# A chunked recurrence whose heads move from chunk-dependent to parity-dependent partitions, with the output normalization queued one chunk later

## The chip, the cores and the metric

The kernel runs on one core of one Trainium2 chip. The metric is the device time of one execution in microseconds (us), the lower the better. All work is in fp32, with bulk matmuls split into a rounded high part and a rest (three matmuls for one product).

## The reference, cut to what matters

Two transformer-like blocks run one after the other on 512 positions of width 1024. The first has an RWKV-7 branch with 8 heads of 64; this recurrence is what the change touches:

```python
def step(state, inp):                     # per head, state S is 64 x 64
    r_t, w_t, k_t, v_t, a_t, b_t = inp
    sa = einsum("bhvk,bhk->bhv", state, a_t)
    state = state * w_t[:, :, None, :] + sa[..., None] * b_t[:, :, None, :] + v_t[..., None] * k_t[:, :, None, :]
    return state, einsum("bhvk,bhk->bhv", state, r_t)
...
y = (y - mu) * rsqrt(var + LN_X_EPS)      # normalized over the 64 of each head
y = y.reshape(bsz, s, D_RWKV) * ln_x_w + ln_x_b
y = y + bonus                             # sum(r * k * r_k) * v per head
return y * g
```

After it come a convolution branch, gates, cross attention to 256 memory rows, an MLP, and the second block (windowed attention, a gated unit, projections).

## The kernel before, in words

The framework orders the instructions of each engine from a plan with estimated durations; each engine then runs its own queue in that order. TensorE's queue therefore mixes the scan's small matmuls with the bulk matmuls (lines 193 to 195) of projections that do not need the scan. Bulk weights are loaded by SyncE's queue (L185), cast on ScalarE (L167) and their rest is formed on VectorE (L168).

The recurrence is computed in 8 chunks of 64 positions, two to a block `tb` of 128. For each chunk `gram` (L441) forms the products within the chunk for all 8 heads; `inverse` (L453) solves the small triangular systems for both chunks of a block on VectorE, 31 steps, with transposes through DRAM (`md`, `M`, `zd`, `ZT`, 16 transfers on SyncE's queue). `chunk` (L490) then goes through these steps, each for 8 heads or 4 head pairs: right-hand sides (L502, and L506 from the carried state), a first solve with 32x32 blocks (L517), the coupling (L521), a second solve (L526), the state update (L533) and the output (L547 from the state, L550 from within the chunk). Between them ScalarE copies right-hand sides out of PSUM (`gsb`), VectorE copies solutions into `VU` and updates the state. `VU` holds values and solutions: for even chunks the values lie on partitions 0 to 63 and the solutions on 64 to 127, for odd chunks the other way round:

```python
kb, ub = 64 * c, 64 * (1 - c)             # c = n % 2
...
PE.matmul(pg[ub:ub + 64, hd * 64:(hd + 1) * 64], lhsT=gr[:, hd, 0:64], rhs=VU[:, tb, c, hd, :], ...)
```

So within a chunk all heads write the same 64 output partitions. An fp32 matmul appears in the trace as two records. `post(tb)` normalizes the output of a block; it follows the block's second chunk. `gt` (gates) takes the result, is transposed at L666 and feeds `ya`. The pool `t` (function `tt`) has ten slots and serves most temporaries.

Of the kernel before, what the change touches and what calls it, by code (L numbers as in the profile page):

```python
# [22 lines left out]
TB = 4  # L23
# [23 lines left out]
def fused_kernel(ctx, tc, a, out):  # L47
# [274 lines left out]
    PC = tp.tile([128, 8, 8], F32, tag="PC", name="PC")  # L322
    G.memset(VU[64:128, :, 0], 0.0)
    G.memset(VU[0:64, :, 1], 0.0)
    bon = tp.tile([128, TB, 8], F32, tag="bon", name="bon")
# [11 lines left out]

    def halves(ap):
        return ap.rearrange("p (m x) -> p m x", x=128)

    def prep(j, tail):
# [7 lines left out]
        for tb in range(TB):  # L349
# [16 lines left out]
        G.tensor_tensor(PC[:, :, 2 * j:2 * j + 2], pp[:, :, 64:65].to_broadcast([128, 8, 2]),  # L366
                        hsel.unsqueeze(1).to_broadcast([128, 8, 2]), op=ALU.mult)
# [13 lines left out]
        kb = KB[:, j].rearrange("p (m x) -> p m x", x=256)  # L381
# [13 lines left out]
    def prep_tail(j, rkk, vs):  # L395
        pb = scbank()
        for tb in range(TB):
            PE.matmul(pb[:, 2 * tb:2 * tb + 2], lhsT=rkk[:, tb * 128:(tb + 1) * 128], rhs=hsel, start=True, stop=True)
        V.tensor_copy(bon[:, :, 2 * j:2 * j + 2], pb[:, 0:8].rearrange("p (t q) -> p t q", q=2))
        pv = scbank()  # L400
        for tb in range(TB):
            PE.transpose(pv[:, tb * 128:(tb + 1) * 128], vs[:, tb * 128:(tb + 1) * 128], ident)
        for c in range(2):
            S.copy(VU[64 * c:64 * c + 64, :, c, 2 * j:2 * j + 2, :],
                   pv[64 * c:64 * c + 64].rearrange("p (t h n) -> p t h n", t=TB, h=2))
# [31 lines left out]
    nc.sync.dma_start(lnx[:, 0], a["ln_x_w"][0:1, :].partition_broadcast(128))  # L437
    nc.sync.dma_start(lnx[:, 1], a["ln_x_b"][0:1, :].partition_broadcast(128))
    lnw, lnb = lnx[:, 0], lnx[:, 1]
    def gram(n):  # L440
        t = reg.tile([128, 8, 128], F32, tag="G4", bufs=4, name=nm("gram"))  # L441
        pq = [scbank(), scbank()]
        for hd in range(8):
            j, p0 = hd // 2, 64 * (hd % 2)
            PE.matmul(pq[hd % 2][:, j * 128:(j + 1) * 128], lhsT=KB[p0:p0 + 64, j, n * 128:(n + 1) * 128],  # L445
                      rhs=AR[p0:p0 + 64, j, n].rearrange("p q c -> p (q c)"), start=True, stop=True)
        tv = t.rearrange("p (j q) c -> p q j c", q=2)
# [5 lines left out]
    def inverse(grams):  # L453
        md = dr.tile([32, 32, 32], F32, tag="md", bufs=2, name=nm("md"))
        for i in range(2):
            ub = 64 * (1 - i)
            for d in range(2):
                q0 = (i * 2 + d) * 8
                nc.sync.dma_start(md[q0:q0 + 8].rearrange("h j i -> j h i"),
                                  grams[i][ub + 32 * d:ub + 32 * d + 32, :, 32 * d:32 * d + 32])  # L460
# [18 lines left out]
        ZT = tt("ZT", (128, 2, 8, 32))  # L479
        for i in range(2):  # L480
            ub = 64 * (1 - i)
            for d in range(2):
                q0 = (i * 2 + d) * 8
                nc.sync.dma_start(ZT[ub + 32 * d:ub + 32 * d + 32, i], zd[q0:q0 + 8].rearrange("h c i -> c h i"))
        return ZT

    state = [None]
    ybank = [None]

    def chunk(n, gr, ZT):  # L490
        tb, c = n // 2, n % 2
        kb, ub = 64 * c, 64 * (1 - c)
        sp = state[0]
# [7 lines left out]
        for hd in range(8):  # L501
            PE.matmul(pg[ub:ub + 64, hd * 64:(hd + 1) * 64], lhsT=gr[:, hd, 0:64],  # L502
                      rhs=VU[:, tb, c, hd, :], start=hd == 0, stop=n == 0 and hd == 7)
        if n > 0:
            for j in range(4):
                PE.matmul(pg[ub:ub + 64, j * 128:(j + 1) * 128], lhsT=AR[:, j, n, 0, :],  # L506
                          rhs=sp[:, j, :], start=False, stop=j == 3)
        if 0 < n < 7:
            spc = tt("spc", (128, 4, 128))
            G.tensor_tensor(spc.rearrange("p j (q v) -> p (j q) v", q=2), sp.rearrange("p j (q v) -> p (j q) v", q=2),  # L510
                            PC[:, n, :].unsqueeze(2).to_broadcast([128, 8, 64]), op=ALU.mult)
        gsb = tt("gsb")
        pu = chbank()
        S.copy(gsb[ub:ub + 32], pg[ub:ub + 32])
        for hd in range(8):
            hs = slice(hd * 64, (hd + 1) * 64)
            PE.matmul(pu[ub:ub + 32, hs], lhsT=ZT[ub:ub + 32, c, hd, :], rhs=gsb[ub:ub + 32, hs],  # L517
                      start=True, stop=True)
        V.tensor_copy(VU[ub:ub + 32, tb, c], pu[ub:ub + 32].rearrange("p (h v) -> p h v", v=64))
        for hd in range(8):  # L520
            PE.matmul(pg[ub + 32:ub + 64, hd * 64:(hd + 1) * 64], lhsT=gr[ub:ub + 32, hd, 32:64],  # L521
                      rhs=VU[ub:ub + 32, tb, c, hd, :], start=False, stop=hd == 7, skip_group_check=True)
        S.copy(gsb[ub + 32:ub + 64], pg[ub + 32:ub + 64])
        for hd in range(8):
            hs = slice(hd * 64, (hd + 1) * 64)
            PE.matmul(pu[ub + 32:ub + 64, hs], lhsT=ZT[ub + 32:ub + 64, c, hd, :], rhs=gsb[ub + 32:ub + 64, hs],  # L526
                      start=True, stop=True)
        V.tensor_copy(VU[ub + 32:ub + 64, tb, c], pu[ub + 32:ub + 64].rearrange("p (h v) -> p h v", v=64))

        if n < 7:  # L530
            pst = chbank()
            for j in range(4):
                PE.matmul(pst[:, j * 128:(j + 1) * 128], lhsT=KBt[:, 2 * j:2 * j + 2, :].rearrange("p h f -> p (h f)"),  # L533
                          rhs=VU[:, tb, c, 2 * j:2 * j + 2, :].rearrange("p h v -> p (h v)"),
                          start=j == 0, stop=j == 3)
            sn = tmp("state", (128, 4, 128), bufs=2)
            V.tensor_tensor(sn.rearrange("p j (q v) -> p (j q) v", q=2), pst.rearrange("p (jq v) -> p jq v", v=64),
                            PC[:, n, :].unsqueeze(2).to_broadcast([128, 8, 64]), op=ALU.mult)
            if n > 0:
                V.tensor_tensor(sn, sn, spc, op=ALU.add)  # L540
            state[0] = sn
        if c == 0:
            ybank[0] = chbank()
        py = ybank[0]
        if n > 0:
            for j in range(4):
                PE.matmul(py[kb:kb + 64, j * 128:(j + 1) * 128], lhsT=AR[:, j, n, 1, :],  # L547
                          rhs=sp[:, j, :], start=j == 0, stop=False)
        for hd in range(8):
            PE.matmul(py[kb:kb + 64, hd * 64:(hd + 1) * 64], lhsT=gr[:, hd, 64:128], rhs=VU[:, tb, c, hd, :],  # L550
                      start=n == 0 and hd == 0, stop=hd == 7)
# [4 lines left out]
    def post(tb):  # L556
        y = tt("y")
        S.copy(y, ybank[0])
        bv = tt("bv")
        for c in range(2):  # L560
            rows = slice(64 * c, 64 * c + 64)
            G.tensor_tensor(heads(bv[rows]), VU[rows, tb, c], bon[rows, tb, :].unsqueeze(2).to_broadcast([64, 8, 64]),
                            op=ALU.mult)
# [38 lines left out]
    scan_front(0)  # L602
    for tb in range(TB):
        if tb < TB - 1:
            scan_front(tb + 1)
        for c in range(2):
# [51 lines left out]
    for j in range(DB):  # L658
# [3 lines left out]
        if j % 2 == 0:  # L662
# [5 lines left out]
            split(p.rearrange("p (j t) -> p j t", t=128), ya[:, :, 0, ts_], ya[:, :, 1, ts_])  # L668
# [511 lines left out]
for _name, _n in VSIZE:  # L1180
# [4 lines left out]
    "mem", "w_lora_w", "w_lora_a", "w_lora_g", "ln_x_w", "ln_x_b", "norm_mem", "norm_final",  # L1185
# [15 lines left out]
def _layout(inputs):  # L1201
# [26 lines left out]
    r["w_v"] = _half_tiles(g["w_kv"][0][:, D:])  # L1228
    w2 = g["w_in_2"][0]
# [27 lines left out]
```

## Time and profile before

| | us |
|---|---|
| median of 3 runs | 1328.11 |
| lowest and highest run | 1325.77, 1330.02 |
| the profiled execution | 1321.5 |
| its span | 1319.5 |
| TensorE busy in it | 1290.2 (98%) |
| VectorE, ScalarE, GpSimd busy | 829.1, 530.4, 166.3 |

A profile shows one execution. Busy time is by engine (PE is TensorE's matmuls, PEld its weight loads, DVE VectorE, ACT ScalarE, POOL GpSimd, SP SyncE); idle time of an engine that is not the bottleneck costs nothing. Matmuls are pipelined: a record's length holds its passage through the array, and the distance from start to start tells what it occupies.

### The profile page before, as it was taken

The page shows a single profiled execution, that of the slowest core. Times are in us where ns is not written, and L with a number is a line of the kernel's source. Part 1 is how long each engine was busy: PE and PEld are TensorE (multiplying, and loading weights), DVE is VectorE, ACT ScalarE, POOL GpSimd, SP SyncE. Part 2 cuts the span into 40 slices and gives each one's busy share as a digit, 9 for nine tenths or more (in the row PEclk, how much of TensorE's full clock was granted, in tenths as well). Part 3 has the DMA queues.
Part 4 walks back from the last instruction along what each step waited for, and adds up shares of the span by engine and source line. Part 5 has one row for each costly group of instructions (what it writes and reads, how often), then busy time and mean ns, then how long its engine had stood idle before and what let it go on. Part 6 is the DMA issues. An engine that isn't in the chain of part 4 may idle for free.

```text
span 1319.5 us, 18273 instructions
## 1 busy us (share of the span) xinstructions
PE 1290.2 (98%) x6594; PEld 1061.5 (80%) x6594; DVE 829.1 (63%) x1657; ACT 530.4 (40%) x956; POOL 166.3 (13%) x178
## 2 busy tenths in 40 slices
PE   8989999999999999999999999999999999999997
PEld 6778888878889888888888888888878777788886
DVE  6867585857477665656845636544677666663356
ACT  6534332322344443544523323324345465333342
POOL 1222101020110020002021020120232000100003
PEclk9989999999999999999999999999999999999999
DMA  6111432323324522143544535323334223233331
GB/s 233 56 56 59 115 102 67 98 59 115 95 66 137 195 98 83 56 161 122 190 128 129 191 97 165 110 92 96 96 120 143 74 70 130 88 96 97 97 118 64
DMA packets 85498, 143.95 MB, mean 109 GB/s; under 512 B 21504, under 2 KB 21632, under 8 KB 85408
## 3 DMA queue, kind: packets, MB, share of 16 engines
q1 hardware_dynamic: 85408, 142.78, 34.7%
q8 instruction: 52, 0.85, 0.3%
q14 instruction: 38, 0.31, 0.1%
HBM read 136.19 MB, written 5.24 MB: 107 GB/s over the span
## 4 chain that ended last, share of the span: by engine, by line
PE 93%; DVE 5%; issue 1%; POOL 0%; DMA 0%; ACT 0%; SPq 0%; DVEq 0%; ACTq 0%; POOLq 0%
PE mm L193 25%; PE mm L194 25%; PE mm L195 25%; PE mm L686 1%; PE mm L687 1%; PE mm L685 1%; PE sc L445 1%; DVE wlo L168 1%; PE ch L1046 1%; PE ch L517 1%; PE ch L1011 1%; PE ch L550 1%; PE ch L521 1%; PE ch L526 1%; PE ch L502 1%
## 5 line engine op out<-in xcount | busy, mean ns | idle before, releaser
L167 ACT CAST whi<-wraw 128x512 fp32r<-128x512 f32 x398 | 246.5, 622 | 518.7 <-PE mm L194 452.8
L168 DVE TENSOR_TENSOR wlo<-wraw,whi 128x512 fp32r<-128x512 f32 x398 | 291.4, 734 | 206.7 <-PE mm L195 105.4
L193 PE MATMUL mm<-h,whi 128*128 128x512 f32 x296 | 118.3, 400 | 0.0
L194 PE MATMUL mm<-h,whi 128*128 128x512 f32 x296 | 117.1, 396 | 0.0
L195 PE MATMUL mm<-h,wlo 128*128 128x512 f32 x296 | 116.6, 394 | 0.0
L193 PE MATMUL mm<-x2g,whi 128*128 128x512 f32 x256 | 100.2, 391 | 0.0
L195 PE MATMUL mm<-x2g,wlo 128*128 128x512 f32 x256 | 99.7, 390 | 0.0
L194 PE MATMUL mm<-x2g,whi 128*128 128x512 f32 x256 | 99.6, 389 | 0.0
L193 PE MATMUL mm<-ff,whi 128*128 128x512 f32 x256 | 99.6, 389 | 0.0
L194 PE MATMUL mm<-ff,whi 128*128 128x512 f32 x256 | 99.6, 389 | 0.0
L195 PE MATMUL mm<-ff,wlo 128*128 128x512 f32 x256 | 99.6, 389 | 0.0
L910 POOL TENSOR_TENSOR X<-X,d 128x512 f32<-128x512 f32 x24 | 39.3, 1636 | 220.9 <-DVE d L908 220.9
L193 PEld LDWEIGHTS mm<-h,whi 128*128 128x128 f32 x296 | 55.9, 189 | 13.6 <-DVE k L287 1.1
L195 PEld LDWEIGHTS mm<-h,wlo 128*128 128x128 f32 x296 | 55.9, 189 | 11.8 <-issue 0.2
L194 PEld LDWEIGHTS mm<-h,whi 128*128 128x128 f32 x296 | 55.9, 189 | 11.2 <-issue 0.2
L716 POOL TENSOR_TENSOR gt<-gt,nsq 128x512 f32<-128x512 f32 x21 | 27.7, 1321 | 274.9 <-ACT nsq L715 267.4
L194 PE MATMUL mm<-h2a,whi 128*128 128x512 f32 x152 | 59.8, 393 | 0.5 <-DVE h2a L933 0.5
L193 PE MATMUL mm<-h2a,whi 128*128 128x512 f32 x152 | 59.4, 393 | 0.3 <-ACT h2a L932 0.3
L195 PE MATMUL mm<-h2a,wlo 128*128 128x512 f32 x152 | 59.7, 393 | 0.0
L193 PE MATMUL mm<-h2b,whi 128*128 128x512 f32 x152 | 59.6, 392 | 0.0
L195 PE MATMUL mm<-h2b,wlo 128*128 128x512 f32 x152 | 59.5, 392 | 0.0
L194 PE MATMUL mm<-h2b,whi 128*128 128x512 f32 x152 | 59.3, 391 | 0.0
(488 smaller groups left out, 2777.7 us busy)
## 6 DMA issues: line engine op xcount, KB each, us to landing
wraw<-in_w_in SPq DMA_DIRECT2D x162, 256.0 KB, 2.7
wraw<-in_w_up SPq DMA_DIRECT2D x64, 256.0 KB, 2.6
wraw<-in_w_down SPq DMA_DIRECT2D x64, 256.0 KB, 2.7
adaraw<-in_w_ada SPq DMA_DIRECT2D x24, 512.0 KB, 3.6
wraw<-in_w_proj_b SPq DMA_DIRECT2D x16, 256.0 KB, 2.6
wraw<-in_w_k SPq DMA_DIRECT2D x16, 256.0 KB, 2.7
wraw<-in_w_proj_a SPq DMA_DIRECT2D x16, 256.0 KB, 2.8
wraw<-in_w_v SPq DMA_DIRECT2D x16, 256.0 KB, 2.7
```

The costliest lines, as they stand in the source:

```text
L167: S.copy(hi, src)
L168: eng.tensor_tensor(lo, src, hi.bitcast(F32), op=ALU.subtract)
L193: PE.matmul(acc, lhsT=wh, rhs=xh, start=start and k == 0, stop=False)
L194: PE.matmul(acc, lhsT=wh, rhs=xl, start=False, stop=False)
L195: PE.matmul(acc, lhsT=wl, rhs=xh, start=False, stop=stop and k == n - 1)
L445: PE.matmul(pq[hd % 2][:, j * 128:(j + 1) * 128], lhsT=KB[p0:p0 + 64, j, n * 128:(n + 1) * 128], rhs=AR[p0:p0 + 64, j, n].rearrange("p q c ...
L502: PE.matmul(pg[ub:ub + 64, hd * 64:(hd + 1) * 64], lhsT=gr[:, hd, 0:64], rhs=VU[:, tb, c, hd, :], start=hd == 0, stop=n == 0 and hd == 7)
L517: PE.matmul(pu[ub:ub + 32, hs], lhsT=ZT[ub:ub + 32, c, hd, :], rhs=gsb[ub:ub + 32, hs], start=True, stop=True)
L521: PE.matmul(pg[ub + 32:ub + 64, hd * 64:(hd + 1) * 64], lhsT=gr[ub:ub + 32, hd, 32:64], rhs=VU[ub:ub + 32, tb, c, hd, :], start=False, sto ...
L526: PE.matmul(pu[ub + 32:ub + 64, hs], lhsT=ZT[ub + 32:ub + 64, c, hd, :], rhs=gsb[ub + 32:ub + 64, hs], start=True, stop=True)
L716: G.tensor_tensor(self.acc, self.acc, sq, op=ALU.add)
L910: G.tensor_tensor(X[:, j], X[:, j], d, op=ALU.add)
```

## The change

Heads are placed by the parity of their pair `j` (pairs 0 and 2 against 1 and 3), for all chunks alike: values of even pairs on partitions 0 to 63 and their solutions on 64 to 127, odd pairs the other way round. Each step's 8 matmuls are issued in `order8`, in which the parity changes from one to the next, so that the output half does too; the free axis of each PSUM tile is 256 columns in place of 512. The first half solution is copied by VectorE and the other by ScalarE. The state is kept in two fixed tiles whose unused blocks are zeroed once; the next chunk's decayed state is formed on GpSimd from the new sum (`cn`). `y` is copied out of PSUM per chunk. The inverse's transfers are split by parity (8 + 4 + 4 + 8 in place of 4 + 4 + 4 + 4). Gate columns and the normalization's weights are laid out by parity on the host, gates are written in four quarter copies, and `post(tb)` is queued after the first chunk of the next block; for the last block it stays behind its second chunk.

```diff
-    VU = reg.tile([128, TB, 2, 8, 64], F32, tag="R", bufs=7, name="VU")
+    VU = reg.tile([128, 8, 8, 64], F32, tag="R", bufs=7, name="VU")
...
-        V.scalar_tensor_tensor(kb[:, :, 64:192], halves(ta), 1.0, halves(m1), op0=ALU.add, op1=ALU.mult)
-        V.tensor_tensor(kb[:, :, 0:64], halves(f)[:, :, 0:64], halves(ip)[:, :, 0:64], op=ALU.mult)
-        V.tensor_tensor(kb[:, :, 192:256], halves(f)[:, :, 64:128], halves(ip)[:, :, 64:128], op=ALU.mult)
+        kb = KB[:, j].rearrange("p (n x) -> p n x", x=128)
+        ub, vb = 64 * (1 - j % 2), 64 * (j % 2)
+        V.scalar_tensor_tensor(kb[:, :, ub:ub + 64], chunks(ta), 1.0, chunks(m1), op0=ALU.add, op1=ALU.mult)
+        V.tensor_tensor(kb[:, :, vb:vb + 64], chunks(f), chunks(ip), op=ALU.mult)
...
-        S.activation(g, p, AF.Copy, scale=0.5)
+        for c in range(2):
+            for jp in range(2):
+                S.activation(g[64 * jp:64 * jp + 64, 256 * c:256 * c + 256],
+                             p[64 * c:64 * c + 64, 256 * jp:256 * jp + 256], AF.Copy, scale=0.5)
...
+    order8 = [(hp, jh, jp) for hp in range(2) for jh in range(2) for jp in range(2)]
...
+        blocks = [(i, d, jp, ((i * 2 + d) * 2 + jp) * 4, 64 * (1 - jp) + 32 * d)
+                  for i in range(2) for d in range(2) for jp in range(2)]
+        for i, d, jp, q0, r0 in blocks:
+            nc.sync.dma_start(md[q0:q0 + 4].rearrange("h j i -> j h i"),
+                              grams[i][r0:r0 + 32, 4 * jp:4 * jp + 4, 32 * d:32 * d + 32])
...
-        for hd in range(8):
-            PE.matmul(pg[ub:ub + 64, hd * 64:(hd + 1) * 64], lhsT=gr[:, hd, 0:64],
-                      rhs=VU[:, tb, c, hd, :], start=hd == 0, stop=n == 0 and hd == 7)
+        for hp, jh, jp in order8:
+            ub, b = 64 * (1 - jp), 2 * jh + hp
+            PE.matmul(pg[ub:ub + 64, b * 64:(b + 1) * 64], lhsT=gr[:, 4 * jp + b, 0:64],
+                      rhs=VU[:, n, 4 * jp + b, :], start=b == 0, stop=n == 0 and b == 3)
...
+        for d in range(2):
+            S.copy(gh[:, d], pg[:, 0:256])
+            for hp, jh, jp in order8:
+                r0, b = 64 * (1 - jp) + 32 * d, 2 * jh + hp
+                hs = slice(b * 64, (b + 1) * 64)
+                PE.matmul(pu[r0:r0 + 32, hs], lhsT=ZT[r0:r0 + 32, c, b, :], rhs=gh[r0:r0 + 32, d, hs],
+                          start=True, stop=True)
+            for jp in range(2):
+                r0 = 64 * (1 - jp) + 32 * d
+                (V.tensor_copy, S.copy)[jp](VU[r0:r0 + 32, n, 4 * jp:4 * jp + 4, :],
+                                            pu[r0:r0 + 32, 0:256].rearrange("p (h v) -> p h v", v=64))
...
+                for hp in range(2):
+                    PE.matmul(pst[64 * hp:64 * hp + 64, j * 64:(j + 1) * 64], lhsT=KBt[:, 2 * j + hp, :],
+                              rhs=VU[:, n, g0 + hp, :], start=j == 0, stop=j == 3)
...
             if n > 0:
-                V.tensor_tensor(sn, sn, spc, op=ALU.add)
-            state[0] = sn
...
+                V.tensor_tensor(s1, ps_, comp[0], op=ALU.add)
+            else:
+                V.tensor_copy(s1, ps_)
+            for hp in range(2):
+                rows = slice(64 * hp, 64 * hp + 64)
+                V.tensor_tensor(sn[rows, :, 64 * hp:64 * hp + 64], s1[rows], pc[rows], op=ALU.mult)
+            if n < 6:
+                cn = tt("cn", (128, 4, 64))
+                G.tensor_tensor(cn, s1, pc, op=ALU.mult)
+                comp[0] = cn
...
+        S.copy(y[:, 256 * c:256 * c + 256], py[:, 0:256])
...
         for c in range(2):
-            chunk(2 * tb + c, grams[tb][c], zts[tb])
-        if tb == TB - 1:
-            mem_norm()
-        post(tb)
+            chunk(2 * tb + c, grams[tb][c], zts[tb], ys[tb])
+            if tb and c == 0:
+                post(tb - 1, ys[tb - 1])
+    mem_norm()
+    post(TB - 1, ys[TB - 1])
```

## Rows read from the trace of the kernel before

**Rows 1.** The page: busy time, share of the span; the chain that ended last.
```profile
PE 1290.2 (98%) x6594; PEld 1061.5 (80%) x6594; DVE 829.1 (63%) x1657; ACT 530.4 (40%) x956; POOL 166.3 (13%) x178
...
PE 93%; DVE 5%; issue 1%; POOL 0%; DMA 0%; ACT 0%; SPq 0%; DVEq 0%; ACTq 0%; POOLq 0%
```

**Rows 2.** Windows: length, busy us of PE, PEld, DVE, ACT, POOL; granted clock, DMA.
```profile
142.00:420.00 278.00, 274.72 (x1925) 230.98 (x1925) 188.76 (x505) 91.00 (x158) 33.08 (x41) 1.00 0.33 95
208.00:232.00 24.00, 23.88 (x252) 20.15 (x253) 11.18 (x19) 5.19 (x9) 6.44 (x10) 1.00 0.17 47
```

**Rows 3.** TensorE groups by shape, 142 to 392 us: tile, shape, records, busy, mean.
```profile
L502 PE MATMUL ch<-VU,gram 128*64 128x64 f32 x128 | 8.8, 222 | 0.0
...
L517 PE MATMUL ch<-gsb,ZT 32*32 32x64 f32 x128 | 8.6, 216 | 0.0
L547 PE MATMUL ch<-state,AR 128*64 128x128 f32 x56 | 7.6, 279 | 0.0
...
L533 PE MATMUL ch<-VU,KBt 128*128 128x128 f32 x56 | 7.4, 274 | 0.0
```

**Rows 4.** TensorE's timeline, 142 to 367 us: start, length, array tile, shape, records.
```profile
142.82 1.16 PE L445 MATMUL sc<-AR,KB 64*128 64x128 f32 x16
...
208.57 1.07 PE L517 MATMUL ch<-gsb,ZT 32*32 32x64 f32 x16
215.03 1.05 PE L533 MATMUL ch<-VU,KBt 128*128 128x128 f32 x8
...
217.93 0.71 PE L506 MATMUL ch<-state,AR 128*64 128x128 f32 x5
218.37 0.32 PE L547 MATMUL ch<-state,AR 128*64 128x128 f32 x1
218.48 0.27 PE L506 MATMUL ch<-state,AR 128*64 128x128 f32 x1
...
218.75 0.71 PE L547 MATMUL ch<-state,AR 128*64 128x128 f32 x5
...
291.00 0.71 PE L445 MATMUL sc<-AR,KB 64*128 64x128 f32 x8
...
298.85 1.10 PE L502 MATMUL ch<-VU,gram 128*64 128x64 f32 x16
301.88 1.09 PE L506 MATMUL ch<-state,AR 128*64 128x128 f32 x8
...
366.42 1.07 PE L517 MATMUL ch<-gsb,ZT 32*32 32x64 f32 x16
```

**Rows 5.** Timeline of weight loads at 218.4 and 1048.3 us.
```profile
218.37 0.14 PEld L506 LDWEIGHTS ch<-state,AR 128*64 128x64 f32 x1
218.37 0.13 PEld L547 LDWEIGHTS ch<-state,AR 128*64 128x64 f32 x1
...
1048.30 0.14 PEld L1046 LDWEIGHTS ch<-apT,vtok 128*64 128x64 f32 x2 [0.36 <-ACT apT L1043]
```

**Rows 6.** VectorE's and ScalarE's groups by shape, 142 to 480 us.
```profile
L528 DVE COPY VU<-ch 32x512 f32<-32x512 f32 x8 | 5.5, 690 | 16.0 <-PE ch L526 16.0
...
L167 ACT CAST Kt<-mm 128x256 fp32r<-128x256 f32 x7 | 2.6, 367 | 0.0
...
L523 ACT COPY gsb<-ch 32x512 f32<-32x512 f32 x8 | 4.6, 578 | 17.6 <-PE ch L521 17.6
```

**Rows 7.** SyncE's timeline of the inverse's last transfers, first and last block.
```profile
184.89 1.82 SPq L484 DMA_DIRECT2D ZT<-zd  x4
...
338.81 1.82 SPq L484 DMA_DIRECT2D ZT<-zd  x4
```

**Rows 8.** By line, the gates' last write and its transposes: lengths, first and last start.
```profile
L577 DVE TENSOR_TENSOR gt<-gt,y x4: 683/692/1750, 242.1 to 400.4; 128x512 f32<-128x512 f32 x4
...
L666 PE MATMUL sc<-ident,gt x16: 272/272/273, 390.6 to 409.5; 128*128 128x128 f32 x16
```

**Rows 9.** Waits, 142 to 392 us: total us, times, longest.
```profile
ACT whi L167 <- PE mm L194: 99.3, 52, 9.1
```

More of the change, by code (lines that the diff above doesn't have):

```diff
@@ L403, in prep_tail @@
         for c in range(2):
-            S.copy(VU[64 * c:64 * c + 64, :, c, 2 * j:2 * j + 2, :],
+            S.copy(VU[vb:vb + 64].rearrange("p (t c) g n -> p c t g n", c=2)[:, c, :, g0:g0 + 2, :],
                    pv[64 * c:64 * c + 64].rearrange("p (t h n) -> p t h n", t=TB, h=2))
@@ L431, in fused_kernel @@
         g = tmp("gt", bufs=4)
[L432 removed]
+        for c in range(2):
+            for jp in range(2):
+                S.activation(g[64 * jp:64 * jp + 64, 256 * c:256 * c + 256],
+                             p[64 * c:64 * c + 64, 256 * jp:256 * jp + 256], AF.Copy, scale=0.5)
         gt.append(g)
     lnx = reg.tile([128, 2, T], F32, tag="Q", bufs=3, name="lnx")
[L437 to L438 removed]
+    for jp in range(2):
+        nc.sync.dma_start(lnx[64 * jp:64 * jp + 64].rearrange("p i x -> p (i x)"),
+                          a["ln_x"][jp:jp + 1, :].partition_broadcast(64))
     lnw, lnb = lnx[:, 0], lnx[:, 1]
+    order8 = [(hp, jh, jp) for hp in range(2) for jh in range(2) for jp in range(2)]
     def gram(n):
@@ L478, in inverse, with chunk @@
             nc.sync.dma_start(zv[k], Z[32 * k:32 * k + 32])
[L479 to L484, printed above, removed]
-        return ZT
[L487 to L493, printed above, removed]
+        ZT = tt("ZT", (128, 2, 4, 32))
+        for i, d, jp, q0, r0 in blocks:
+            nc.sync.dma_start(ZT[r0:r0 + 32, i], zd[q0:q0 + 4].rearrange("h c i -> c h i"))
+        return ZT
+    states = [tmp("state", (128, 4, 128), bufs=2) for _ in range(2)]
+    for st in states:
+        G.memset(st, 0.0)
+    comp = [None]
+    def chunk(n, gr, ZT, y):
+        c = n % 2
+        sp, sn = states[(n + 1) % 2], states[n % 2]
         pt = scbank()
@@ L504, in chunk @@
         if n > 0:
             for j in range(4):
[L506 to L528, printed above, removed]
+                ub, jh = 64 * (1 - j % 2), j // 2
+                PE.matmul(pg[ub:ub + 64, jh * 128:(jh + 1) * 128], lhsT=AR[:, j, n, 0, :],
+                          rhs=sp[:, j, :], start=False, stop=jh == 1)
@@ new lines, in chunk @@
+        for d in range(2):
[5 more added lines that the diff above has]
+                          start=True, stop=True)
+            for jp in range(2):
+                r0 = 64 * (1 - jp) + 32 * d
+                (V.tensor_copy, S.copy)[jp](VU[r0:r0 + 32, n, 4 * jp:4 * jp + 4, :],
+                                            pu[r0:r0 + 32, 0:256].rearrange("p (h v) -> p h v", v=64))
+            if d == 0:
+                for hp, jh, jp in order8:
+                    ub, b = 64 * (1 - jp), 2 * jh + hp
+                    PE.matmul(pg[ub + 32:ub + 64, b * 64:(b + 1) * 64], lhsT=gr[ub:ub + 32, 4 * jp + b, 32:64],
+                              rhs=VU[ub:ub + 32, n, 4 * jp + b, :], start=False, stop=b == 3, skip_group_check=True)
@@ L532, in chunk @@
             for j in range(4):
[L533 to L538, printed above, removed]
@@ L545, in chunk @@
+        py = chbank()
         if n > 0:
             for j in range(4):
[L547 to L551, printed above, removed]
+                vb, jh = 64 * (j % 2), j // 2
+                PE.matmul(py[vb:vb + 64, jh * 128:(jh + 1) * 128], lhsT=AR[:, j, n, 1, :],
+                          rhs=sp[:, j, :], start=jh == 0, stop=False)
@@ L553, in heads, with post @@
+        for hp, jh, jp in order8:
+            vb, b = 64 * jp, 2 * jh + hp
+            PE.matmul(py[vb:vb + 64, b * 64:(b + 1) * 64], lhsT=gr[:, 4 * jp + b, 64:128], rhs=VU[:, n, 4 * jp + b, :],
+                      start=n == 0 and b == 0, stop=b == 3)
+        S.copy(y[:, 256 * c:256 * c + 256], py[:, 0:256])
     def heads(ap):
         return ap.rearrange("p (h v) -> p h v", v=64)
-    def post(tb):
-        y = tt("y")
-        S.copy(y, ybank[0])
+    def post(tb, y):
         bv = tt("bv")
[L560 to L563, printed above, removed]
+        bvv = bv.rearrange("p (c b v) -> p c b v", c=2, v=64)
+        ns = slice(2 * tb, 2 * tb + 2)
+        for jp in range(2):
+            rows = slice(64 * jp, 64 * jp + 64)
+            G.tensor_tensor(bvv[rows], VU[rows, ns, 4 * jp:4 * jp + 4, :],
+                            bon[rows, ns, :].unsqueeze(3).to_broadcast([64, 2, 4, 64]), op=ALU.mult)
@@ L667, in fused_kernel @@
             ts_ = slice(tb * 128, (tb + 1) * 128)
-            split(p.rearrange("p (j t) -> p j t", t=128), ya[:, :, 0, ts_], ya[:, :, 1, ts_])
+            yav = [ya[:, :, i, ts_].rearrange("p j (c t) -> p j c t", c=2) for i in range(2)]
+            split(p.rearrange("p (c j t) -> p j c t", c=2, t=64), yav[0], yav[1])
     merged = [regionr("merged0"), regionr("merged1")]
@@ L1228, in _layout, with by_parity @@
     r["w_v"] = _half_tiles(g["w_kv"][0][:, D:])
+    def by_parity(w):
+        return w.reshape(-1, 2, 2, 128).transpose(0, 2, 1, 3).reshape(-1, 2, 256)
+    r["w_lora_g"] = np.ascontiguousarray(by_parity(g["w_lora_g"][0]).reshape(1, -1, 512))
+    r["ln_x"] = np.ascontiguousarray(np.concatenate(
+        [np.tile(by_parity(g[n])[0], (1, 2)) for n in ("ln_x_w", "ln_x_b")], axis=1))
     w2 = g["w_in_2"][0]
```

41 lines of the change are left out of this document (19 added, 22 removed).

## The prediction

> **What bounds the kernel now.** I read the page first: TensorE is busy for 98% of the span and carries 93% of the chain that ended last [rows 1]. Then the windows over the stretch that the change touches, 142 to 420 us, from the first Gram products to the end of the memory keys: TensorE is busy for 274.7 of 278 us at the full granted clock, and for 23.88 of 24 us while a pair of chunks runs [rows 2]. So there is no wait worth removing: bulk projections stand in the same queue between the scan's steps and fill them. What counts is how long TensorE itself is occupied by the scan's small matmuls; a shorter chain through VectorE or ScalarE alone is worth at most the 3.3 us in which TensorE idles there. The view by shape then gives the number of scan records, two for each fp32 matmul [rows 3], and the timeline how closely they follow each other [rows 4].
>
> **What TensorE pays for the scan now.** In each chunk the eight heads' matmuls of a step all write the same 64 (or 32) output partitions. A step of 16 records with 64 columns takes 1.07 to 1.10 us, so (1.07 - 0.21)/15 = 57 ns from start to start; a step of 8 records with 128 columns takes 1.09 us or 1.05 us, some 111 to 117 ns apart [rows 4]. Where consecutive matmuls use different parts of the array, the same trace shows them side by side: the Gram matmuls alternate between the two row halves, and 16 records of 128 columns take 1.16 us, which is (1.16 - 0.27)/15 = 59 ns each, and 8 take 0.71 us [rows 4]. L506 and L547 write different column halves, and where the one follows the other, L547 starts at 218.37 us while L506 goes on until 218.48 and later, so that the 16 records from 217.93 to 219.46 us take 1.53 us against about 2.0 us (1.09 + 1.09 less the overlap of two neighbours, 0.16) [rows 4]. That overlap of some 0.45 us occurs four times in the scan: 1.8 us that the kernel has already.
>
> **The change part by part.** The new order alternates the pair's parity, hence the output half, from matmul to matmul in every step.
> - L517, L521 and L526 (three steps, 8 chunks, 128 records each [rows 3]): 24 steps of 32x32 tiles, now at two diagonal places. With the Gram's ratio (117/59, nearly 2) the spacing falls from 57 to 30 ns, a step from 1.07 to 0.21 + 15 x 0.03 = 0.66 us: 0.40 us each, 9.6 us in all. If two such tiles cannot run together: 0.
> - L506 and L547 (56 records each, 14 steps): 1.09 to 0.71 us, 0.38 us each, 5.3 us, less the 1.8 us already had: 3.5 us.
> - L502 and L550 (128 records each, 16 steps, 64 columns, 128 rows): 0.40 us each, 6.4 us. L533 turns from 8 records of 128 columns (1.05 us) into 16 of 64 columns at alternating halves, 0.22 + 15 x 0.03 = 0.67 us: 0.38 us in 7 chunks, 2.7 us. Together 9.1 us.
>
> These 9.1 us need two weight loads of 64 columns at once, since alone such loads follow each other no faster than the matmuls do. From below: if they stay one behind the other, the spacing stays 57 ns and L533 costs 0.05 us more in each chunk, -0.4 us. From above: 9.1 us. I take 9.1, because L1046 later in the kernel alternates column halves over all 128 rows, and there two loads together take 0.14 us while one alone takes 0.13; L506's and L547's loads also both start at 218.37 us [rows 5]. TensorE: Matmul & The Clock Gate of the Trainium skill, section Part 3: Packing small matmuls, says that a weight load overlaps matmuls in flight only where the row group differs. The trace disagrees, by the same rows and by L502, whose loads for the same rows run behind its matmuls at a 58 ns spacing. By the page the sum would be 13.1 us, by the rows 22.2.
>
> The sum on TensorE is 9.6 + 3.5 + 9.1 = 22.2 us.
>
> Edits off TensorE. VectorE and ScalarE copies shrink from 512 to 256 columns (0.69 and 0.58 us now, a 128x256 cast takes 0.37 us [rows 6]); one half of each solution copy goes to ScalarE, so the two halves run side by side. The state update becomes one add and two half-height products, and ScalarE gets one y copy per chunk in place of one per pair. All this is under TensorE's bulk work; were that cover gone, the chain of a chunk would still be shorter than now. Four scaled copies replace one for each gate tile: about 4 x 0.37 - 0.58 = 0.9 us more of ScalarE for each of four tiles, with the six bulk matmuls of each tile as cover; two multiplies for KB become one. I count these at nothing. The inverse issues 24 transfers where it issued 16: 8 more of about 0.45 us on SyncE's queue (1.82 us for four [rows 7]), 3.6 us later for each of four inverses and for the weight loads queued behind them. The cover: the last inverse's transfers are issued at 338.81 us, land some 4 us after, and are first used at 366.42 us; the first ones are issued at 184.89 and used at 208.57 us [rows 4, 7]. Without that cover it would cost up to 14.4 us. The output normalization moves behind the next pair's first chunk. It has no TensorE work; on GpSimd, which is busy for 33 of 278 us [rows 2], its products stand ahead of the next carried-state product, which is wanted a whole chunk later, and on VectorE its ops stand ahead of the second chunk's copies. Its result is read at 390.6 us at the earliest, and the last one, which does not move relative to its chunk, is ready at 401.1 us and read by the last transposes around 409 us [rows 8].
>
> Against this I put 2 us of new TensorE waits: the copy halves on ScalarE stand in one queue with the weight casts, which wait for TensorE 52 times in this stretch [rows 9], and 16 such halves are new. The bounds are 0 and about 10 us (16 times one cast of 0.62 us). Net: -20 us.
>
> **The rivals.**
> - *Two row halves in one bank.* In the steps of 32x32 tiles the two tiles sit in different row halves and write the same PSUM bank, at other partitions. No row of the trace has that: the Gram's halves write two banks, and L1046's column halves write one bank but use the same rows. If they exclude each other, 9.6 us are lost: 22.2 - 9.6 - 2 = 10.6 us gained, 1317.5 us. TensorEngine Tiling (Array Packing) of the Trainium skill, Restrictions and Gotchas, says exactly this of row tiles and PSUM banks; no row here tests it for tiles with different output partitions. For the gain speaks that L1046's two halves of one bank do run together.
> - *Serial weight loads* for 128-row tiles: 9.5 us lost, 10.7 us gained, 1317.4 us; the loads of [rows 5] speak against it.
> - *A floor on records.* No stretch of this trace shows records closer than some 55 ns on average. If that is a limit of issue, only the L506/L547 steps gain: 3.5 - 0.4 - 2 = 1.1 us, 1327 us. Against it: pairs that start together, as at 218.37 us.
> - *Waits eat half.* The ten us of the upper bound above: about 1316 us.
> - *Slower.* Two y tiles, gh, s1 and the carried product live at once in the ten-slot work pool, where the inverse needs Z and a new product tile for each of 31 steps; if it has to wait for slots, the last inverse comes late. It has about 24 us of margin, and TensorE gains 20 us; so it must be late by more than 24 + 20 + 4 = 48 us to make the kernel slower by 4 us, and costs 1 us for each beyond. At 55 us late the time is 1328 - 20 + 31 = 1339 us.
>
> **How the numbers follow.** The profiled execution took 1321.5 us (span 1319.5), 6.6 us below the median of the three runs, 1328.11. The sum is a difference in TensorE occupancy, so I apply it to both: about 1301.5 us for a profile, 1308 us for the median. Chances: forecast 0.50; one of the two half-gains missing 0.25; waits eat half 0.09; record floor 0.09; slower 0.07. A change under 0.3% (4 us) cannot be told from none here. Faster by more is then 0.84, same 0.09, slower 0.07. The range: with no new waits and 3 to 6 us more from the idle time and from step borders it reaches down to 1300; upward it takes in the three cases near 1317 and reaches 1320.
>
> **What the profile after would show.** L517, L521 and L526 at about 0.66 us for 16 records; if they stay at 1.07, the bank rule holds. L502, L550 and L533 at about 0.67 us; 1.1 us means serial loads. Both unchanged means a floor. TensorE idle over the scan should stay below 6 us; more, released by ScalarE copies, is the wait rival, and a gap ahead of a pair's first L517 released by ZT's transfers is the slower one. The prediction is wrong if TensorE's total busy time between the first Gram and the first use of ya shrinks by under 10 us.

## The result, and the profile after

The changed kernel takes 1317.76 us (median of 4 runs, 1315.0 to 1318.49) against 1327.83 (4 runs, 1325.77 to 1330.02) for the kernel before beside it: a ratio of 0.993, 95% interval [0.991, 0.9951]. It is faster, by 10 us where 20 were forecast. The profiled execution took 1317.51 us, with a span of 1315.8.

The page of the changed kernel, which answers to [rows 1]: TensorE still sets the time.

```profile
PE 1280.6 (97%) x6650; PEld 1044.5 (79%) x6650; DVE 826.6 (63%) x1665; ACT 536.5 (41%) x988; POOL 165.6 (13%) x180
...
PE 93%; DVE 4%; issue 1%; ACT 1%; DMA 0%; POOL 0%; SPq 0%; DVEq 0%; ACTq 0%; POOLq 0%
```

TensorE's timeline in the changed kernel, which answers to [rows 4] (L520 is what was L517 and L526, L529 was L521, L508 was L502, L513 was L506):

```profile
148.86 0.69 PE L508 MATMUL ch<-VU,gram 128*64 128x64 f32 x16
...
213.25 0.64 PE L520 MATMUL ch<-gh,ZT 32*32 32x64 f32 x16
214.68 0.29 PE L529 MATMUL ch<-VU,gram 32*32 32x64 f32 x2
215.56 0.63 PE L529 MATMUL ch<-VU,gram 32*32 32x64 f32 x14
...
222.23 0.66 PE L513 MATMUL ch<-state,AR 128*64 128x128 f32 x8
```

A step takes 0.64 to 0.69 us where it took 1.07 to 1.10, as forecast. But L529 is no longer one step: two records, bulk work, then fourteen. The groups by shape, 142 to 420 us, show what that does to the sums. L520 takes 10.6 us where L517 and L526 took 8.6 each; L508 and L513 are 3 us down. L529 fell only from 8.6 to 7.6 us, L537 (was L533) only from 7.4 to 6.9, and the Gram products (L451, was L445), which the change hardly touches, rose from 13.7 to 16.8. One of their steps lies in the stretch of lower clock shown below; in the last kernel of the experiments, where none does, they still take 15.8, and why is open.

```profile
L451 PE MATMUL sc<-AR,KB 64*128 64x128 f32 x128 | 16.8, 303 | 0.8 <-DVE gram L455 0.8
L520 PE MATMUL ch<-gh,ZT 32*32 32x64 f32 x256 | 10.6, 223 | 0.0
L529 PE MATMUL ch<-VU,gram 32*32 32x64 f32 x128 | 7.6, 222 | 2.5 <-DVE VU L524 2.5
...
L537 PE MATMUL ch<-VU,KBt 128*64 128x64 f32 x112 | 6.9, 247 | 0.0
L508 PE MATMUL ch<-VU,gram 128*64 128x64 f32 x128 | 5.9, 225 | 0.0
...
L513 PE MATMUL ch<-state,AR 128*64 128x128 f32 x56 | 4.6, 285 | 4.1 <-DVE state L548 4.1
```

The windows, which answer to [rows 2] (length, busy us of PE, PEld, DVE, ACT, POOL; granted clock, DMA share, GB/s):

```profile
142.00:420.00 278.00, 269.09 (x2011) 216.62 (x2010) 192.09 (x520) 99.44 (x192) 32.02 (x41) 0.98 0.34 96
284.00:288.00 4.00, 2.91 (x33) 2.17 (x34) 3.73 (x9) 1.32 (x3) 2.43 (x3) 1.00 0.00 0
288.00:292.00 4.00, 4.00 (x41) 3.14 (x41) 1.95 (x7) 0.37 (x1) 0.00 (x0) 0.69 0.12 21
292.00:296.00 4.00, 4.00 (x37) 3.12 (x38) 1.99 (x6) 0.36 (x1) 1.39 (x2) 0.50 0.18 66
344.00:348.00 4.00, 2.55 (x27) 1.49 (x23) 3.63 (x13) 1.41 (x3) 1.60 (x1) 0.94 0.25 74
348.00:352.00 4.00, 4.00 (x25) 2.80 (x25) 1.16 (x3) 0.39 (x2) 1.29 (x1) 0.63 0.00 0
```

TensorE now idles for 8.9 us of the stretch where it idled for 3.3, and the clock, full over the stretch in the first profile of before, is granted at 0.50 to 0.69 in places: part or all of such a place runs at 1.2 GHz in place of 2.4. The mean of 0.98 alone is no sign of the change, since a second profile of the kernel before has it too (below). In both places shown, TensorE has idled for 1.1 and 1.45 us of 4 just before, while VectorE was busy for 3.6 to 3.7. The waits of TensorE say on what:

```profile
PE ch L513 <- DVE state L548: 4.1, 5, 1.4
PE ch L529 <- DVE VU L524: 2.5, 2, 1.4
```

In the kernel before the scan waited for the state once (groups by shape; L506 is now L513):

```profile
L506 PE MATMUL ch<-state,AR 128*64 128x128 f32 x56 | 7.5, 276 | 1.3 <-DVE state L540 1.3
```

And the timeline of the other engines at one of the waits for the copy: the normalization of the pair before (on VectorE L149 to L154, on GpSimd L574 and L576) is under way, and its VectorE operations stand ahead of the solution copy (L524) that TensorE waits for. An operation on 128x8 elements beside a GpSimd product takes 1.23 us; its neighbours of that size take 0.17.

```profile
344.01 1.60 POOL L576 TENSOR_TENSOR bv<-bv,lnx 128x512 f32<-128x512 f32 x1
344.40 1.23 DVE L149 TENSOR_SCALAR rq_v<-yv 128x8 f32<-128x8 f32 x1
...
345.67 0.17 DVE L150 TENSOR_SCALAR rq_y<-rq_v 128x8 int32<-128x8 int32 x1
345.87 0.42 DVE L524 COPY VU<-ch 32x256 f32<-32x256 f32 x1
...
346.32 0.36 ACT L524 COPY VU<-ch 32x256 f32<-32x256 f32 x1 [2.62 <-DVE VU L524]
```

The last two rows also show that the halves of a solution copy do not run side by side: ScalarE's starts when VectorE's has ended. That is so 14 of 16 times (waits of ScalarE):

```profile
ACT VU L524 <- DVE VU L524: 19.2, 14, 2.7
```

### The profile page after: what moved, and what is told of

Read it like the earlier page. It is cut to its first block, busy times and chain, and to the rows that moved or that the text cites. A ratio compares the mean times of both kernels' runs of the same rounds, so it can differ in the third digit from the quotient of the medians.

```text
span 1315.8 us, 18480 instructions
## 1 busy us (share of the span) xinstructions
PE 1280.6 (97%) x6650; PEld 1044.5 (79%) x6650; DVE 826.6 (63%) x1665; ACT 536.5 (41%) x988; POOL 165.6 (13%) x180
## 4 chain that ended last, share of the span: by engine, by line
PE 93%; DVE 4%; issue 1%; ACT 1%; DMA 0%; POOL 0%; SPq 0%; DVEq 0%; ACTq 0%; POOLq 0%
PE mm L194 25%; PE mm L193 25%; PE mm L195 25%; PE mm L703 1%; PE mm L702 1%; PE mm L701 1%; PE sc L451 1%; PE ch L1062 1%; PE ch L520 1%; DVE wlo L168 1%; DVE state L548 1%; PE ch L1027 1%; PE ch L529 1%; PE sc L1058 0%; PE ch L193 0%
## 5 line engine op out<-in xcount | busy, mean ns | idle before, releaser
L194 PE MATMUL mm<-h,whi 128*128 128x512 f32 x296 | 119.4, 403 | 0.0
L193 PE MATMUL mm<-h,whi 128*128 128x512 f32 x296 | 118.8, 401 | 0.0
L194 PEld LDWEIGHTS mm<-h,whi 128*128 128x128 f32 x296 | 56.5, 191 | 12.4 <-issue 0.7
L732 POOL TENSOR_TENSOR gt<-gt,nsq 128x512 f32<-128x512 f32 x21 | 27.7, 1320 | 276.1 <-ACT nsq L731 268.6
```

What stands on the lines that cost most here:

```text
L193: PE.matmul(acc, lhsT=wh, rhs=xh, start=start and k == 0, stop=False)
L194: PE.matmul(acc, lhsT=wh, rhs=xl, start=False, stop=False)
L732: G.tensor_tensor(self.acc, self.acc, sq, op=ALU.add)
```

## The experiments

Two theories stood at the start. *Queue*: the placement is worth what its steps show, and the moved normalization takes part of it back through VectorE's queue. *Cover*: the shorter steps themselves cover less of VectorE's chain, and the normalization is innocent.

**The normalization back behind its pair's second chunk**, all else as changed.

```diff
-            if tb and c == 0:
-                post(tb - 1, ys[tb - 1])
-    mem_norm()
-    post(TB - 1, ys[TB - 1])
+        if tb == TB - 1:
+            mem_norm()
+        post(tb, ys[tb])
```

> The changed kernel with the normalization queued behind the pair's second chunk again, as before the change; nothing else differs. The queue theory (the moved normalization's VectorE and GpSimd work stands ahead of the scan's copies, TensorE waits at L529 and L513 and its clock falls afterwards) expects 3 to 7 us less than the changed kernel, about 1312 us, with TensorE idle over the scan back under 6 us. The cover theory (the waits come only because the steps that hid the state update now take half as long) expects the same time as the changed kernel within 2 us.

Measured: 1311.45 us (1310.39 to 1313.05), ratio 0.9889 [0.9869, 0.991]. The move costs the changed kernel some 6 us; cover alone falls. But not all new waits go: waits on the copy, 2.5 us, shrink to 0.4, those on the state stay.

```profile
PE ch L513 <- DVE state L548: 4.3, 6, 2.1
...
PE ch L529 <- DVE VU L524: 0.4, 1, 0.4
```

To exclude a difference between chips, both ran once more on one chip.

> The changed kernel itself, on the same chip as the next three kernels. The theory that the moved normalization costs about 6 us expects it 5 to 7 us above the kernel in which only that move is taken back (so far these two were timed on different chips, 1317.8 and 1311.5 us). If that difference was one of chips, the two lie within 2 us of each other here.

> The changed kernel with the normalization back behind its pair's second chunk. About 1311 us, 15 to 16 us under the kernel before. In the program's order TensorE changes 109 times between tile shapes from the first Gram product to the last gate transposes, and 167 times between source lines, against 83 and 133 in the kernel before.

Measured: 1317.45 us (1313.19 to 1319.16) as changed, 1312.74 (1309.11 to 1312.95) with the normalization back: 4.7 us. The move costs about 5 to 6 us.

**Only the normalization moved**, in the kernel before.

```diff
-        if tb == TB - 1:
-            mem_norm()
-        post(tb)
+            if c:
+                S.copy(ys[tb], ybank[0])
+            if tb and c == 0:
+                post(tb - 1, ys[tb - 1])
+    mem_norm()
+    post(TB - 1, ys[TB - 1])
```

> The kernel before with one part of the change alone: the normalization (but not the copy of y out of PSUM) queued behind the first chunk of the next pair. The queue theory expects 1 to 5 us more than before, since the chain of the second chunk gets the normalization's work ahead of it, with less harm than in the changed kernel as the steps still take twice as long and cover more; the cover theory expects no change within 2 us.

Measured: 1335.21 us (1333.27 to 1337.97), ratio 1.0066 [1.0043, 1.0088]: 7.9 us slower. Alone, too, the move costs. Here most of it shows as clock: in its windows TensorE is 2.6 us less busy than before over the stretch, and the mean clock is 0.95. At 384 us the waits come first; at 284 us the clock is down with TensorE busy for 4.00 of 4 us.

```profile
142.00:420.00 278.00, 272.10 (x1820) 226.40 (x1819) 185.18 (x486) 83.75 (x144) 35.22 (x41) 0.95 0.30 86
284.00:288.00 4.00, 4.00 (x24) 3.00 (x24) 0.68 (x1) 0.50 (x1) 0.00 (x0) 0.59 0.00 0
384.00:388.00 4.00, 2.25 (x23) 1.51 (x20) 3.97 (x5) 0.47 (x1) 3.85 (x4) 1.00 0.00 0
392.00:396.00 4.00, 4.00 (x22) 2.99 (x22) 0.13 (x2) 0.58 (x1) 0.00 (x0) 0.50 0.02 4
```

**Moved, but with its four GpSimd operations on VectorE.**

```diff
-            G.tensor_tensor(bvv[rows], VU[rows, ns, 4 * jp:4 * jp + 4, :], ...)
+            V.tensor_tensor(bvv[rows], VU[rows, ns, 4 * jp:4 * jp + 4, :], ...)
...
-        G.tensor_tensor(bv, bv, lnb, op=ALU.add)
+        V.tensor_tensor(bv, bv, lnb, op=ALU.add)
...
-        G.tensor_tensor(y, y, lnw, op=ALU.mult)
+        V.tensor_tensor(y, y, lnw, op=ALU.mult)
```

> The changed kernel, normalization moved as in the change, but its four GpSimd ops per block on VectorE. If the moved normalization costs time because GpSimd's ops slow VectorE's in the chain of the scan (a 128x8 op took 1.23 us beside one), this gains 2 to 5 us against the changed kernel, to 1313 to 1316 us. If it costs because of its place in VectorE's queue, four more ops of 0.4 to 0.7 us make it the same or slower, 1317 to 1322 us.

Measured: 1315.99 us (1313.84 to 1317.3), ratio 0.9924 [0.9903, 0.9945]: no different from the changed kernel. The wait for the state halves (2.1 us), L529 no longer waits for the copy, and L149 takes 0.17 us in all four blocks, so GpSimd's overlap did stretch VectorE's work; but VectorE's longer queue now delays the memory's normalization, and TensorE waits there instead:

```profile
PE sc L659 <- DVE mt L612: 6.5, 1, 6.5
```

**The matmuls grouped by output half**, with everything else as changed: the same placement without the alternation.

```diff
-    order8 = [(hp, jh, jp) for hp in range(2) for jh in range(2) for jp in range(2)]
+    order8 = [(hp, jh, jp) for jp in range(2) for hp in range(2) for jh in range(2)]
...
-            for j in range(4):              # carried state, output of the state
+            for j in (0, 2, 1, 3):
...
-            for j in range(4):              # state products
...
-                for hp in range(2):
+            for hp in range(2):
+                for j in range(4):
...
```

> The changed kernel with every step's matmuls grouped by output half (four of one half, then four of the other) instead of alternating. If the gain of the steps comes from the alternation, steps of 16 records go back towards 1.07 us, less what the engine's look-ahead across the border of the two groups saves (about 0.2 us a step), and the time rises by 10 to 18 us, to some 1330 us. If the placement by parity alone is enough, because the engine looks far enough ahead, the steps stay near 0.66 us and the time is unchanged within 2 us.

Measured: 1330.61 us (1328.82 to 1334.17), ratio 1.0037 [1.002, 1.0053], 13 us above the changed kernel. Without the order the gain in time is gone, but the steps do not go back to what they were (TensorE's timeline): two groups of eight records take 0.88 to 0.92 us, between 0.64 and 1.07. Of the 13 us about half is clock: with each run's lost clock taken off, as further down, 7 us are left.

```profile
212.90 0.88 PE L520 MATMUL ch<-gh,ZT 32*32 32x64 f32 x16
...
220.57 0.92 PE L508 MATMUL ch<-VU,gram 128*64 128x64 f32 x16
```

**Both halves of the solution copy on VectorE.**

```diff
-                (V.tensor_copy, S.copy)[jp](VU[r0:r0 + 32, n, 4 * jp:4 * jp + 4, :], ...)
+                V.tensor_copy(VU[r0:r0 + 32, n, 4 * jp:4 * jp + 4, :], ...)
```

> The changed kernel with both halves of each solution copy on VectorE. The prediction took the two halves to run side by side; the trace after shows ScalarE's half starting when VectorE's ends. If that is the rule, one engine doing both costs 0.06 us more a copy and saves ScalarE's queue: same time within 2 us. If ScalarE's queue behind weight casts is a real part of the waits, it gains 2 us or more; if the halves do overlap in most chunks, it loses 2 to 5 us.

Measured: 1316.62 us (1313.94 to 1320.35), ratio 0.993 [0.9908, 0.9952]: the same. ScalarE's share of the copy gives nothing and costs nothing.

**The carried product (`cn`) on VectorE**, with the normalization back.

```diff
-                G.tensor_tensor(cn, s1, pc, op=ALU.mult)
+                V.tensor_tensor(cn, s1, pc, op=ALU.mult)
```

> The version with the normalization back in its place (x1_post_back), and the carried product cn on VectorE behind the two state products, not on GpSimd beside them. In the changed kernel one 64x256 state product takes 0.70 us on average while GpSimd works on cn, where 256 columns take 0.42 us elsewhere on VectorE. If the two engines get in each other's way, the state products fall to 0.42 us, TensorE's wait ahead of L513 falls from 4.3 to under 2.5 us and the time by 1.5 to 4 us against x1_post_back (to some 1309 us). If the wait is only the shorter cover, the products stay as long and the time changes by less than 1.5 us.

Measured: 1311.81 us (1306.24 to 1314.45), ratio 0.9892 [0.9867, 0.9916]: no gain that shows over the spread. The wait for the state fell from 4.3 to 2.0 us, yet the mean of the fourteen state products stayed (579 ns; 567 with `cn` on GpSimd, 698 in the changed kernel). The mean hides what happened. In the changed kernel a chunk's two products run beside `cn`:

```profile
282.03 1.17 DVE L548 TENSOR_TENSOR state<-s,PC 64x256 f32<-64x256 f32 x2
282.08 0.84 POOL L551 TENSOR_TENSOR cn<-s,PC 128x256 f32<-128x256 f32 x1 [38.24 <-DVE s L543]
```

With `cn` on VectorE another GpSimd product, the normalization's L574, starts earlier and takes its place in three of seven chunks; in the other four GpSimd is idle beside them:

```profile
335.08 1.60 DVE L548 TENSOR_TENSOR state<-s,PC 64x256 f32<-64x256 f32 x2
335.13 2.46 POOL L574 TENSOR_TENSOR bv<-VU,bon 64x512 f32<-64x512 f32 x2 [32.85 <-DVE s L543]
...
345.92 0.85 DVE L548 TENSOR_TENSOR state<-s,PC 64x256 f32<-64x256 f32 x2
```

So GpSimd's products do stretch them, from 0.84 or 0.85 us for the two to 1.17 and 1.60, and the edit put one in place of another. All three waits that are left (0.31, 0.86 and 0.86 us) stand behind the stretched ones; behind the four others TensorE does not wait.

**No split step.** In TensorE's queue of the changed kernel the eight matmuls of L529 stand as one and seven, in all eight chunks: the first reads the half that VectorE copies, which is ready earlier. Starting with the other half makes them one step. This is built on the kernel with the normalization back, where L529 stands in the same two pieces.

```diff
-                for hp, jh, jp in order8:
+                for hp, jh, jq in order8:
+                    jp = 1 - jq
```

> x1_post_back with the coupling step L529 starting with the parity whose half ScalarE copies last, so that its 8 matmuls stand together in TensorE's queue instead of 1 and 7 with bulk matmuls between. If each such interruption costs TensorE about 0.2 us (a change of tile shape in and out), eight of them are worth 1.6 us, and the time falls by 1 to 2 us against x1_post_back; if the wait only moves, no change.

> The same with the eight matmuls that subtract the first half's part of the solution starting at the parity that ScalarE copies: they are queued together, and the changes of tile shape fall from 109 to 94. If a border between shapes costs TensorE about 0.1 us, 1.5 us less than the kernel of the normalization moved back; if the later start of the step costs as much as the borders give, the same time.

Measured: 1309.17 us (1305.86 to 1311.76), ratio 0.9877 [0.9852, 0.9903]; and on the chip on which the kernel with the normalization back took 1312.74, 1306.40 (1305.28 to 1307.95), ratio 0.9855 [0.9826, 0.9884]. So 2 us between chips, 6 on one chip, where 1.5 were expected. The two differ by the clock of the runs: with each run's lost clock taken off (further down) it is 3 us in both. What a split costs, from TensorE's timeline with it:

```profile
343.86 0.40 PE L193 MATMUL mm<-h,whi 128*128 128x512 f32 x1
344.19 0.29 PE L529 MATMUL ch<-VU,gram 32*32 32x64 f32 x2
344.41 0.50 PE L194 MATMUL mm<-h,whi 128*128 128x512 f32 x1
344.75 0.39 PE L195 MATMUL mm<-h,wlo 128*128 128x512 f32 x1
344.98 0.40 PE L193 MATMUL mm<-h,whi 128*128 128x512 f32 x1
345.31 0.63 PE L529 MATMUL ch<-VU,gram 32*32 32x64 f32 x14
345.87 0.50 PE L194 MATMUL mm<-h,whi 128*128 128x512 f32 x1
```

and without:

```profile
213.00 0.40 PE L193 MATMUL mm<-h,whi 128*128 128x512 f32 x1
...
213.33 0.64 PE L530 MATMUL ch<-VU,gram 32*32 32x64 f32 x16
...
213.90 0.50 PE L194 MATMUL mm<-h,whi 128*128 128x512 f32 x1
```

Bulk matmuls follow each other at 0.23 us (344.75 to 344.98). Split, the step puts (344.41 - 343.86 - 0.23) + (345.87 - 344.98 - 0.23) = 0.98 us between them; whole, 213.90 - 213.00 - 0.23 = 0.67. That is 0.31 us more. The bulk matmul behind a piece also delays the next one, by 0.34 - 0.23 = 0.11 us (344.41 to 344.75), as it does behind a whole step (213.90 to 214.23), and a split step has one such place more. So a split costs some 0.42 us, eight of them 3.4 us.

**The state products whole as well** (L537 stood as two and six in all seven chunks).

```diff
-            for j in range(4):
+            for j in (1, 0, 3, 2):
-                              ..., start=j == 0, stop=j == 3)
+                              ..., start=j == 1, stop=j == 2)
```

> The same again with the state products also starting at the parity that is copied last, so that they too are queued together: 87 changes of tile shape and 133 of source line, as many as the kernel before. If the borders are the rest of the gap between the gain on paper (22 us) and the 16 us measured, 2 to 2.5 us less than the kernel of the normalization moved back, near 1309 us; if they are not, within 1 us of it.

Measured: 1306.79 us (1304.53 to 1308.76), ratio 0.9856 [0.9826, 0.9887]: no further gain in the time over the 1306.40 us, though its steps are now as short as the sum had them (groups by shape; L562 was L550 and as changed L561, L558 was L547 and L557, L530 was L529, L538 was L537):

```profile
L562 PE MATMUL ch<-VU,gram 128*64 128x64 f32 x128 | 5.5, 223 | 0.0
...
L530 PE MATMUL ch<-VU,gram 32*32 32x64 f32 x128 | 5.1, 217 | 0.2 <-ACT VU L524 0.2
L538 PE MATMUL ch<-VU,KBt 128*64 128x64 f32 x112 | 4.8, 228 | 0.0
...
L558 PE MATMUL ch<-state,AR 128*64 128x128 f32 x56 | 4.3, 275 | 0.0
```

**The kernel before, profiled again**, to see how far one program's profiles differ.

> The kernel before, unchanged, profiled a second time. Its first profile shows the full granted clock over the whole scan and took 1321.5 us, 6 us under the median of its runs. If spells of the lower clock come and go between executions of one program, this profile shows some between 142 and 420 us and a time nearer 1328 us; if its clock is full again, the median's 6 us have another cause.

Measured: 1327.25 us, against 1321.5 in the first profile. TensorE is as busy; the clock is not the same (compare [rows 2]):

```profile
142.00:420.00 278.00, 274.71 (x1906) 230.59 (x1905) 185.03 (x498) 89.53 (x155) 33.08 (x41) 0.98 0.32 93
224.00:228.00 4.00, 4.00 (x24) 2.90 (x21) 0.00 (x0) 0.58 (x1) 0.90 (x3) 0.53 0.00 0
```

## Why the prediction was right in its mechanism and wrong in its size

Each profile can be taken apart. Idle time of TensorE from 142 to 420 us is the length less PE's busy time. Time lost to the clock is summed over the windows of 2 us in which TensorE is busy, each as its length times (1 - granted clock), from 0 to 420 us (with 1.7 us more behind it in the changed kernel, at 1032 to 1038 us, and in the grouped one). What is left of a difference in time is TensorE's occupancy: time gained against the first profile of before, plus what idle and clock took in addition. Before against itself comes out at 1.1, which is how far the method can be trusted.

| kernel | profiled time | idle | lost to clock | occupancy gained |
|---|---|---|---|---|
| before | 1321.5 | 3.3 | 3.7 | 0 |
| before, again | 1327.25 | 3.3 | 10.5 | 1.1 |
| changed | 1317.51 | 8.9 | 12.5 | 18.4 |
| normalization back (again) | 1311.71 | 6.9 | 8.1 | 17.8 |
| and no split (again) | 1306.95 | 7.1 | 6.7 | 21.3 |
| and state products whole | 1304.53 | 7.7 | 4.9 | 22.6 |
| grouped | 1334.17 | 6.1 | 23.6 | 10.0 |
| before, normalization moved | 1337.73 | 5.9 | 16.9 | -0.4 |

The timed runs bear the table out. Each lists its span and mean granted clock; with span times (1 - clock) taken off, the means are 1314.2 us for before (40 runs beside the experiments), 1301.8 as changed (11), 1299.8 with the normalization back (10), 1296.9 without the split (10), 1295.6 with the state products whole (4), 1308.8 grouped (10) and 1317.5 for before with the normalization moved (6). The differences to before, 12.4, 14.4, 17.3, 18.6, 5.4 and -3.3 us, agree within 0.5 us with the table's occupancy less the added idle time, but for grouped (7.2 there). What was taken off is 11.5 us for before, 14.8 as changed and 11.9 with the normalization back; 1.5 to 3 us of it lie at the end of the span, where TensorE has finished.

So of the 20.2 us forecast (22.2 less 2) some 10 are missing: 3.8 of occupancy (18.4 in place of 22.2), 3.6 of waits (5.6 in place of 2) and about 3 of clock, which the forecast took to be the same on both sides.

- **The mechanism was right.** 22.2 us less occupancy was the sum; 22.6 is what the kernel without split steps has, and its groups agree: the scan's steps together fell from 66.1 us (three of 8.6, then 8.8, 9.0, 7.4, 7.5 and 7.6) to 39.6 (L520 10.2, L530 5.1, L508 5.1, L513 4.6, L538 4.8, L558 4.3, L562 5.5). Of these 26.5 us, 10.5 are in L517, L521 and L526 (9.6 forecast), 6.2 in L506 and L547 (5.3, before the overlap was taken off) and 9.8 in L502, L550 and L533 (9.1). The sums fall by more than the occupancy does, as they count overlaps of neighbouring steps twice and leave out the 2.1 us by which the Gram products rose. By its own sign, too, the prediction stands: TensorE's busy time from the first Gram product to the first use of `ya` fell by 12.2 us as changed (266.4 to 254.2), and 10 was the limit.
- **The bank rival fell.** Sixteen records on two diagonal 32x32 tiles that write one bank take 0.64 us, not 1.07. TensorEngine Tiling (Array Packing) of the Trainium skill, Restrictions and Gotchas, says that different row tiles cannot use the same PSUM bank at one time; the measurement decides otherwise for these tiles, which lie in different columns as well and write different partitions.
- **The serial-loads rival and the record floor fell.** L508, with 128 rows, takes 0.69 us, so its records stand (0.69 - 0.22)/15 = 31 ns apart. The sentence of TensorE: Matmul & The Clock Gate of the Trainium skill, Part 3: Packing small matmuls, that a load overlaps matmuls in flight only where the row group differs, is not borne out here.
- **Where luck came in.** The bank and the serial-loads rival named 1317.5 and 1317.4 us, within 0.4 us of the measured time, and neither happened. The upper end of the range, 1320, came from them and from the wait rival, so that it holds the measured time is no merit of the sum.
- **The step that failed first: the moved normalization, for which the sum has no term.** The reason given was that it "has no TensorE work"; that "its ops stand ahead of the second chunk's copies" was written down and not priced. TensorE waits for those copies. The move costs 5 to 6 us as timed in the changed kernel and 7.9 in the kernel before. In the profiles, 1317.51 - 1311.71 = 5.8 us are 2.0 of idle time and 4.4 of clock, less 0.6 of occupancy; over the timed runs they are 2.0 us of work and waits and 2.9 of clock. That the waits at 284 and 344 us bring the clock down is what the windows suggest; but it also falls in busy stretches, and how the move leads to it there stays open.
- **The second: "24 steps", each taken whole.** The sum priced every step as 16 records in a row. The copy in two halves lets the plan queue one or two matmuls as soon as the first half is there, so L529 and L537 stand in two pieces, and what is behind them too (L561, L557). That is 18.4 in place of 22.6 us of occupancy. Timed, undoing the split of L529 gives 2 to 6 us, 3 of them without the clock. Taking both the move and this split back gives 1306.4 us, where 1308 was forecast; that is in part luck, since some 17 of the 21 us are occupancy and waits and the rest is clock.
- **The new waits, 2 us, were 5.6,** and not where they were put: none over 0.6 us was released by ScalarE. So the waits-eat-half rival names nearly the measured time, with a mechanism that did not happen. Of the 5.6 us, 2.0 go with the normalization and 3.6 stay without it: the wait for the state (4.1 us as changed, 4.3 with the normalization back, 4.6 without splits) rose from 1.3. Two things meet in it. With the normalization back, five of the six waits stand behind state products that GpSimd stretches (1.17 us or more for the two), and where GpSimd is idle beside them, in four chunks with `cn` on VectorE, TensorE does not wait. But in the grouped kernel, whose steps are longer, three such stretched pairs (1.17 and 1.18 us) cause no wait either. So the cover theory holds in part: the shorter steps bare a stretch that longer ones hide. The sixth wait (2.15 us) is in the last chunk, where the kernel before waited for 1.3.
- **That "the chain of a chunk would still be shorter than now" was wrong** where these waits arise. The state update takes 0.42 + 1.17 us beside `cn` where it took 0.69 + 0.68, and the halves of a solution copy run one behind the other, 0.42 + 0.36 us where one copy took 0.69.
- **Held:** no late inverse, and no wait of TensorE in the stretch that names ZT or a slot of the work pool. That ScalarE's half of the copy costs nothing held as well (1316.62 us without it), but it gives nothing either.
- **The base.** Applying the sum "to both", the profile and the median, hid 6.8 us: the first profile of before lost 3.7 us to the clock up to 420 us, the second 10.5, which more than covers the 5.75 us between their times. The sum fits a profile and a median alike only where both lose the same to the clock.

## What to carry to other kernels

Small fp32 matmuls that alternate between halves of the array cost little more than half here (0.64 to 0.69 us a step in place of 1.07 to 1.10), and the whole gain comes only while a step stays one run in TensorE's queue: when an operand is copied in parts, start the step with the part that arrives last. Work that has no TensorE instructions of its own is not free when it is put ahead of a copy that TensorE waits for; price it by what it delays on that queue, at its duration beside the engines that will then be busy. A mean over operations can hide which neighbour stretched them; look at them one by one. Before two profiles are subtracted, take out idle time and lost clock, since one program's own profiles differed by 6.8 us in clock alone.

## What the runs showed of the hardware that was not expected

- Grouped by half, the two groups of eight still take 0.88 to 0.92 us in place of 1.07 to 1.10: about half of the occupancy gain (10.0 of 18.4 us) comes with the placement alone, without the alternation.
- A small VectorE operation (128x8) took 1.23 us beside a GpSimd product and 0.17 without; the two state products of a chunk (64x256 each) took 0.84 us together with GpSimd idle, 1.17 beside `cn` and 1.60 to 2.25 beside the normalization's L574.
- The granted clock was 0.53 over 4 us in which TensorE was busy throughout, in a scan that ran at 1.00 in another execution of the same program. What decides that, no run here shows.
